# Splitting two early weight chunks in pieces and reordering the last product of a hybrid block

## The chip, the cores and the metric

The program runs on one core of a Trainium2 chip. The metric is device time in microseconds of one execution. All weights come from HBM in fp32, and the whole block is one launch.

## What is computed

One block over 256 tokens of width 2048: a SwiGLU layer of width 5632, a mixer (an S5 scan beside a gated spatial unit, with gates and an output product), and a second SwiGLU layer, each added to the residual, then a last norm:

```python
h = rms_norm(x, ffn1_norm)
x = x + 0.5 * ((silu(h @ ffn1_w_gate) * (h @ ffn1_w_up)) @ ffn1_w_down)
h = rms_norm(x, mix_norm)
...
x = x + merged @ w_out
h = rms_norm(x, ffn2_norm)
x = x + 0.5 * ((silu(h @ ffn2_w_gate) * (h @ ffn2_w_up)) @ ffn2_w_down)
return rms_norm(x, final_norm)
```

The change touches the first microseconds of the first `h @ ffn1_w_gate`, `h @ ffn1_w_up`, and the last microseconds of the last `@ ffn2_w_down` with the final norm behind it.

## The kernel before, in words

**Three products for one.** TensorE works on fp32r operands, which hold fewer bits than fp32. So each fp32 number is split into a high part (`hi`, the number rounded to fp32r) and a low part (`lo`, the rest), and a product is the sum of three matmuls: hi by hi, hi by lo, lo by hi (lines 216 to 218). The weights are split while the program runs: `split_piece` (line 147) has ScalarE (ACT) write `whi` from `raw`, and then VectorE (DVE) write `wlo` as `raw - whi`.

**Chunks.** All weights come as a list of chunks of 128 x 2048 fp32 (1 MiB) in the order in which the products use them. A chunk holds four pieces of 128 x 512. One piece with 128 rows of the input is a step of six matmuls of 512 columns: three for each half of the 256 tokens (`step`, line 212). So a chunk is 24 matmuls. There are three buffers for `raw`, three for `whi` and three for `wlo`.

**What sets the order.** Each engine works off its instructions in the order of the code. `take` (line 193) hands out one piece; ahead of each it calls `tick` (line 174), which first runs hooks set for this tick, then what is pending (`pend`, the evictions of finished products, put there by `job`, line 220), and at the first piece of a chunk calls `split_to` for the chunk two ahead, which queues that chunk's load on SP and its split on ACT and DVE.

**The start** (lines 746 to 796). The first chunk is loaded and split in four pieces, so that the first matmuls can start as soon as a quarter of it is there. The second and third chunks are split whole, between the splits of the input `xT` (`split_h1`, two of the sixteen k blocks at a time). The first eight chunks, `w1s`, hold gate and up pieces in turn, two k blocks to a chunk.

**The end** (`down_out`, line 1043). The last product has 12 k blocks (`kt`) and four column blocks of 512. Three of them run as usual, by `job`. The eviction of each (`evac`, line 1053) is on DVE an addition to `x_sb` (line 294) and two products with the last norm's gain (line 1051), and on ACT two sums of squares (line 273); the third also loads ACT's table for the square root (line 1061). The fourth column block is taken in one go, all 12 pieces first (line 1067); then for each token half `h` come its 36 matmuls (lines 1072 to 1074), the addition (line 1076), its square, gain and norm, and the stores. Both halves' sums stand in one accumulator tile `acc` of 128 x 2 x 512; the pool `ps` has three such tiles.

Of the kernel before, what the change touches and what calls it, by code (L numbers as in the profile page):

```python
# [13 lines left out]
ALU = mybir.AluOpType  # L14
# [12 lines left out]
SUB = 2048  # L27
# [18 lines left out]
def f(ap):  # L46
    return ap.bitcast(F32)
# [3 lines left out]
def kernel(  # L51
# [31 lines left out]
    act, dve, pe, pool = nc.scalar, nc.vector, nc.tensor, nc.gpsimd  # L83
# [55 lines left out]
    def load_to(i):  # L139
        while st["load"] <= min(i, NSUB - 1):  # L140
            j = st["load"]
            t = wp.tile([P, SUB], F32, tag="raw", name="raw", bufs=NRAW)
            nc.sync.dma_start(out=t, in_=chunks[j])
            raws[j] = t
            st["load"] += 1

    def split_piece(hi, lo, r, s):
        act.activation(out=hi[:, s], in_=r[:, s], func=AF.Copy)  # L148
        dve.tensor_tensor(out=lo[:, s], in0=r[:, s], in1=f(hi[:, s]), op=ALU.subtract)  # L149

    def split_to(i):
        while st["split"] <= min(i, NSUB - 1):
            j = st["split"]
            load_to(j + NRAW - 1)
            r = raws.pop(j)
            hi = wp.tile([P, SUB], F32R, tag="whi", name="whi", bufs=NSPL)
            lo = wp.tile([P, SUB], F32R, tag="wlo", name="wlo", bufs=NSPL)
            split_piece(hi, lo, r, slice(0, SUB))
            splits[j] = (hi, lo)
            st["split"] += 1  # L160

    pend = []
# [4 lines left out]
    def at(delta, fn):  # L167
        hooks.setdefault(st["tick"] + delta, []).append(fn)
# [5 lines left out]
    def tick():  # L174
        for fn in hooks.pop(st["tick"], ()):
            fn()
        while pend:
            pend.pop(0)()
        if st["off"] == 0:
            split_to(st["sub"] + LOOK)  # L180
            splits.pop(st["sub"] - 1, None)
        credit[0] += credit[1]
        while fillers and credit[0] >= 1.0:
            try:
                next(fillers[0])
                credit[0] -= 1.0
            except StopIteration:
                fillers.pop(0)
        if not fillers:
            credit[0] = 0.0  # L190
        st["tick"] += 1

    def take(n):
        if st["off"] % N == 0:
            tick()
        hi, lo = splits[st["sub"]]
        a = st["off"]
        st["off"] += n
        if st["off"] == SUB:
            st["off"] = 0  # L200
            st["sub"] += 1
        return hi[:, a:a + n], lo[:, a:a + n]
# [6 lines left out]
    def new_acc():  # L209
        return ps.tile([P, 2, N], F32, tag="acc", name="acc")  # L210
# [9 lines left out]
    def job(lhs, kt, evac):  # L220
        acc = new_acc()
        for k in range(kt):
            step(acc, lhs, k, k == 0, k == kt - 1)
        pend.append(lambda: evac(acc))
# [15 lines left out]
    def small():  # L240
        return ev.tile([P, 8], F32, tag="sm", name="sm", bufs=2)
# [5 lines left out]
    def split_gain(dst, src, g, k):  # L247
        act.activation(out=dst[:, 0, :], in_=src, func=AF.Copy, scale=g[:, k:k + 1])
        dve.scalar_tensor_tensor(out=dst[:, 1, :], in0=src, scalar=g[:, k:k + 1],
                                 in1=f(dst[:, 0, :]), op0=ALU.mult, op1=ALU.subtract)  # L250
# [20 lines left out]
    def square(m, h):  # L271
        j = ev.tile([P, N], BF16, tag="junk", name="junk", bufs=1)
        act.activation(out=j, in_=x_sb[:, h, m * N:m * N + N], func=AF.Square,  # L273
                       accum_out=ssq[:, h, m:m + 1])

    def rms(hs=slice(0, 2)):
        r = ev.tile([P, 2], F32, tag="rc", name="rc", bufs=2)[:, hs]
        s = small()
        n = hs.stop - hs.start
        dve.tensor_reduce(out=s[:, 0:n], in_=ssq[:, hs, :], axis=AX.X, op=ALU.add)  # L280
        rsqrt(r, s[:, 0:n], D, s[:, 2:2 + n])
        return r
# [9 lines left out]
    def add_residual(acc, m, scale):  # L292
        xs = x_sb[:, :, m * N:m * N + N]
        dve.scalar_tensor_tensor(out=xs, in0=acc, scalar=scale, in1=xs, op0=ALU.mult, op1=ALU.add)  # L294
# [477 lines left out]
    def split_h1(k0):  # L772
        for k in (k0, k0 + 1):
            split_gain(h1[:, k], xT[:, k, :], g1, k)
# [15 lines left out]
    splits[0] = (hi0, lo0)  # L790
    st["split"] = 1
    split_h1(2)
    split_to(1)
    split_h1(4)
    for i in range(5):
        at(2 + 3 * i, lambda i=i: split_h1(2 * i + 6))

# [246 lines left out]
    def down_out(gt, kt):  # L1044
        fin = hp.tile([P, 3, D], F32, tag="h", name="fin")
        xg, gf_sb = fin[:, 0:2, :], fin[:, 2, :]
        pool.dma_start(out=gf_sb, in_=gf.to_broadcast([P, D]))

        def gained(m, h):
            s = slice(m * N, m * N + N)  # L1050
            dve.tensor_tensor(out=xg[:, h, s], in0=x_sb[:, h, s], in1=gf_sb[:, s], op=ALU.mult)

        def evac(m):
            def go(acc):
                add_residual(acc, m, 0.5)
                for h in range(2):
                    square(m, h)
                for h in range(2):
                    gained(m, h)
                if m == 2:  # L1060
                    act.activation(out=small()[:, 0:1], in_=eps_t, func=AF.Sqrt)
            return go

        for m in range(3):
            job(gt, kt, evac(m))
        acc = new_acc()
        pieces = [take(N) for _ in range(kt)]
        c3 = slice(3 * N, 4 * N)
        for h in range(2):
            t = slice(h * P, h * P + P)  # L1070
            for k, (hi, lo) in enumerate(pieces):
                pe.matmul(acc[:, h, :], lhsT=gt[:, k, 0, t], rhs=hi, start=k == 0, stop=False)
                pe.matmul(acc[:, h, :], lhsT=gt[:, k, 0, t], rhs=lo, start=False, stop=False)
                pe.matmul(acc[:, h, :], lhsT=gt[:, k, 1, t], rhs=hi, start=False, stop=k == kt - 1)
            xs = x_sb[:, h, c3]
            dve.scalar_tensor_tensor(out=xs, in0=acc[:, h, :], scalar=0.5, in1=xs, op0=ALU.mult, op1=ALU.add)
            square(3, h)
            gained(3, h)
            r = rms(slice(h, h + 1))
            for i, eng in enumerate((dve, act, dve, act)):  # L1080
                o = xg[:, h, i * N:(i + 1) * N]
                if eng is dve:
                    dve.tensor_scalar(out=o, in0=o, scalar1=r, scalar2=None, op0=ALU.mult)
                    nc.sync.dma_start(out=out[:, h, i * N:(i + 1) * N], in_=o)
                else:
                    act.activation(out=o, in_=o, func=AF.Copy, scale=r)
                    act.dma_start(out=out[:, h, i * N:(i + 1) * N], in_=o)

    ffn(h3, gp2, down_out)
    gp2.release()  # L1090
    h3p.release()
# [88 lines left out]
```

## Time and profile before

| | |
|---|---|
| median of 3 runs | 2055.1 us (2053.28 to 2055.16) |
| profiled execution | 2053.59 us, its span 2051.8 us |
| mean granted TensorE clock | 0.995 |
| busy: PE, DVE, ACT, POOL | 2027.8, 1127.6, 865.0, 72.8 us |
| read from HBM | 398.21 MB, 200 GB/s over the span |

The profile is one execution. PE is TensorE's matmuls, PEld its weight loads, SP the engine whose queue issues the weights' DMAs. The granted clock is 1.00 at 2.4 GHz and 0.50 at 1.2 GHz. A row of the timeline gives the start in us from the beginning of the span, the duration, the engine and line, what is written and read, the shape, and in brackets the idle time of the engine before it with what ended it. Matmuls overlap: one lasts some 0.39 us, while the next starts some 0.23 us after it.

### The profile page before, as it was taken

The numbers are of one execution on the slowest core, as the hardware profiler recorded it, in microseconds if no ns is written. First come the engines' busy times: TensorE is split into PE (matmuls) and PEld (weight loads), VectorE is DVE, ScalarE is ACT, GpSimd is POOL, SyncE is SP. The second block draws the span as 40 slices with busy tenths as digits, with TensorE's granted clock in tenths as the row PEclk, the third lists the DMA queues.
The fourth block names the chain that finished last, engine by engine and source line by source line (L and its number), as shares of the span: only waits on it lengthen the run. The fifth ranks groups of instructions, "written<-read, shape, count | busy, mean of one in ns | idle before, by whom it ended". The sixth has DMA issues, their size and how long they took to land.

```text
span 2051.8 us, 23150 instructions
## 1 busy us (share of the span) xinstructions
PE 2027.8 (99%) x9764; PEld 1676.7 (82%) x9764; DVE 1127.6 (55%) x1102; ACT 865.0 (42%) x705; POOL 72.8 (4%) x134
## 2 busy tenths in 40 slices
PE   9999999999999999989999999999999999999997
PEld 7888888888888888878888888888888888888886
DVE  5765565555664555546765665544444444444454
ACT  6543334444334454434435444533433443333343
POOL 0000000111000000011100000000000000000000
PEclk9999999999999999999999999999999999999999
DMA  7557665565665455557765455555555555555552
GB/s 310 198 195 226 231 240 209 196 216 204 209 208 192 174 195 198 213 178 247 236 227 210 175 185 188 210 187 186 193 196 185 190 188 197 186 200 188 185 190 98
DMA packets 66489, 412.20 MB, mean 201 GB/s; under 512 B 10272, under 2 KB 10928, under 8 KB 20560
## 3 DMA queue, kind: packets, MB, share of 16 engines
q1 hardware_dynamic: 53280, 378.56, 52.0%
q0 software_dynamic: 10656, 27.93, 4.3%
q10 hardware_dynamic: 2448, 4.22, 0.6%
q8 instruction: 76, 1.25, 0.2%
q14 instruction: 29, 0.24, 0.0%
HBM read 398.21 MB, written 12.45 MB: 200 GB/s over the span
## 4 chain that ended last, share of the span: by engine, by line
PE 97%; DVE 1%; ACT 1%; issue 1%; DMA 0%; SPq 0%; ACTq 0%
PE acc L216 31%; PE acc L218 30%; PE acc L217 30%; PE q L258 2%; ACT whi L148 1%; PE q L588 0%; PE q L724 0%; PE acc L234 0%; PE acc L233 0%; PE acc L232 0%; DMA raw<-in_w1s_dram 0%; DVE wlo L149 0%; PE q L681 0%; PE q L885 0%; PE q L721 0%
## 5 line engine op out<-in xcount | busy, mean ns | idle before, releaser
L149 DVE TENSOR_TENSOR wlo<-raw,whi 128x2048 fp32r<-128x2048 f32 (+1 forms) x359 | 815.7, 2274 | 810.2 <-ACT whi L148 810.0
L148 ACT ACTIVATE whi<-raw 128x2048 fp32r<-128x2048 f32 (+1 forms) x359 | 682.2, 1901 | 913.2 <-PE acc L218 835.0
L216 PE MATMUL acc<-whi,h 128*128 128x512 f32 x1856 | 728.0, 392 | 1.2 <-ACT whi L148 1.2
L217 PE MATMUL acc<-wlo,h 128*128 128x512 f32 x1856 | 723.8, 390 | 2.2 <-DVE wlo L149 2.0
L218 PE MATMUL acc<-whi,h 128*128 128x512 f32 x1856 | 723.4, 390 | 0.0
L217 PEld LDWEIGHTS acc<-wlo,h 128*128 128x128 f32 x1856 | 349.2, 188 | 74.3 <-DVE wlo L149 3.2
L216 PEld LDWEIGHTS acc<-whi,h 128*128 128x128 f32 x1856 | 349.1, 188 | 74.2 <-ACT whi L148 1.6
L218 PEld LDWEIGHTS acc<-whi,h 128*128 128x128 f32 x1856 | 349.1, 188 | 73.0
L216 PE MATMUL acc<-whi,gt 128*128 128x512 f32 x680 | 266.1, 391 | 0.0
L218 PE MATMUL acc<-whi,gt 128*128 128x512 f32 x680 | 266.1, 391 | 0.0
L217 PE MATMUL acc<-wlo,gt 128*128 128x512 f32 x680 | 265.1, 390 | 0.0
L217 PEld LDWEIGHTS acc<-wlo,gt 128*128 128x128 f32 x680 | 127.7, 188 | 27.6
L218 PEld LDWEIGHTS acc<-whi,gt 128*128 128x128 f32 x680 | 127.7, 188 | 27.1
L216 PEld LDWEIGHTS acc<-whi,gt 128*128 128x128 f32 x680 | 127.7, 188 | 26.6
L319 ACT ACTIVATE t<-acc,rc 128x512 f32<-128x512 f32 x44 | 27.9, 686 | 63.4 <-PE acc L218 63.4
L216 PE MATMUL acc<-whi,mT 128*128 128x512 f32 x128 | 50.2, 392 | 0.0
L294 DVE SCALAR_TENSOR_TENSOR x_sb<-acc,x_sb 128x1024 f32<-128x1024 f32 x27 | 33.1, 1225 | 30.9 <-PE acc L218 30.9
L218 PE MATMUL acc<-whi,mT 128*128 128x512 f32 x128 | 49.9, 389 | 0.0
L217 PE MATMUL acc<-wlo,mT 128*128 128x512 f32 x128 | 49.8, 389 | 0.0
L273 ACT ACTIVATE junk<-x_sb 128x512 bf16<-128x512 f32 x32 | 20.2, 631 | 66.2 <-DVE x_sb L294 53.0
L329 DVE SCALAR_TENSOR_TENSOR t<-acc,rc,t 128x512 f32<-128x512 f32 x44 | 31.0, 745 | 16.8 <-PE acc L218 16.8
L244 ACT ACTIVATE gt<-q 128x512 fp32r<-128x512 f32 x44 | 23.9, 596 | 29.1 <-PE q L258 29.1
(200 smaller groups left out, 1067.3 us busy)
## 6 DMA issues: line engine op xcount, KB each, us to landing
raw<-in_w1d_dram SPq DMA_DIRECT2D x44, 1024.0 KB, 4.9
raw<-in_w2g_dram SPq DMA_DIRECT2D x44, 1024.0 KB, 4.8
raw<-in_w2u_dram SPq DMA_DIRECT2D x44, 1024.0 KB, 4.8
raw<-in_w2d_dram SPq DMA_DIRECT2D x44, 1024.0 KB, 4.8
raw<-in_w1g_dram SPq DMA_DIRECT2D x40, 1024.0 KB, 4.8
raw<-in_w1u_dram SPq DMA_DIRECT2D x40, 1024.0 KB, 4.9
raw<-in_w_in_dram SPq DMA_DIRECT2D x24, 1024.0 KB, 4.8
raw<-in_w_gb_dram SPq DMA_DIRECT2D x16, 1024.0 KB, 5.3
```

The source lines that it names most:

```text
L148: act.activation(out=hi[:, s], in_=r[:, s], func=AF.Copy)
L149: dve.tensor_tensor(out=lo[:, s], in0=r[:, s], in1=f(hi[:, s]), op=ALU.subtract)
L216: pe.matmul(acc[:, h, :], lhsT=lhs[:, k, 0, t], rhs=hi, start=first, stop=False)
L217: pe.matmul(acc[:, h, :], lhsT=lhs[:, k, 0, t], rhs=lo, start=False, stop=False)
L218: pe.matmul(acc[:, h, :], lhsT=lhs[:, k, 1, t], rhs=hi, start=False, stop=last)
L244: act.activation(out=dst[:, :, 0, :], in_=src, func=AF.Copy)
L258: pe.transpose(q[:, i, h * P:h * P + P], src[:, h, c:c + P], ident)
L273: act.activation(out=j, in_=x_sb[:, h, m * N:m * N + N], func=AF.Square, accum_out=ssq[:, h, m:m + 1])
L294: dve.scalar_tensor_tensor(out=xs, in0=acc, scalar=scale, in1=xs, op0=ALU.mult, op1=ALU.add)
L319: act.activation(out=s[:, h, :], in_=acc[:, h, :], func=AF.Silu, scale=rc(h))
L329: dve.scalar_tensor_tensor(out=s[:, h, :], in0=acc[:, h, :], scalar=rc(h), in1=s[:, h, :], op0=ALU.mult, op1=ALU.mult)
```

## The change

`split_to` gets a number of parts. The second chunk is split in four parts of 512 columns, the third in two of 1024 (its call now stands ahead of the first product; before, the first tick made it, at the same place of the order). In the last product, the eviction of the third column block is taken out of `pend` while the twelve pieces are taken, and run behind them. Each token half gets an accumulator tile of its own.

```diff
--- before.py
+++ after.py
@@ -148,14 +148,16 @@
         act.activation(out=hi[:, s], in_=r[:, s], func=AF.Copy)
         dve.tensor_tensor(out=lo[:, s], in0=r[:, s], in1=f(hi[:, s]), op=ALU.subtract)
 
-    def split_to(i):
+    def split_to(i, parts=1):
         while st["split"] <= min(i, NSUB - 1):
             j = st["split"]
             load_to(j + NRAW - 1)
             r = raws.pop(j)
             hi = wp.tile([P, SUB], F32R, tag="whi", name="whi", bufs=NSPL)
             lo = wp.tile([P, SUB], F32R, tag="wlo", name="wlo", bufs=NSPL)
-            split_piece(hi, lo, r, slice(0, SUB))
+            w = SUB // parts
+            for p in range(parts):
+                split_piece(hi, lo, r, slice(p * w, p * w + w))
             splits[j] = (hi, lo)
             st["split"] += 1
 
@@ -790,8 +792,9 @@
     splits[0] = (hi0, lo0)
     st["split"] = 1
     split_h1(2)
-    split_to(1)
+    split_to(1, 4)
     split_h1(4)
+    split_to(2, 2)
     for i in range(5):
         at(2 + 3 * i, lambda i=i: split_h1(2 * i + 6))
 
@@ -1063,17 +1066,21 @@
 
         for m in range(3):
             job(gt, kt, evac(m))
-        acc = new_acc()
+        late = list(pend)
+        pend.clear()
         pieces = [take(N) for _ in range(kt)]
+        for fn in late:
+            fn()
         c3 = slice(3 * N, 4 * N)
         for h in range(2):
             t = slice(h * P, h * P + P)
+            acc = new_acc()[:, 0, :]
             for k, (hi, lo) in enumerate(pieces):
-                pe.matmul(acc[:, h, :], lhsT=gt[:, k, 0, t], rhs=hi, start=k == 0, stop=False)
-                pe.matmul(acc[:, h, :], lhsT=gt[:, k, 0, t], rhs=lo, start=False, stop=False)
-                pe.matmul(acc[:, h, :], lhsT=gt[:, k, 1, t], rhs=hi, start=False, stop=k == kt - 1)
+                pe.matmul(acc, lhsT=gt[:, k, 0, t], rhs=hi, start=k == 0, stop=False)
+                pe.matmul(acc, lhsT=gt[:, k, 0, t], rhs=lo, start=False, stop=False)
+                pe.matmul(acc, lhsT=gt[:, k, 1, t], rhs=hi, start=False, stop=k == kt - 1)
             xs = x_sb[:, h, c3]
-            dve.scalar_tensor_tensor(out=xs, in0=acc[:, h, :], scalar=0.5, in1=xs, op0=ALU.mult, op1=ALU.add)
+            dve.scalar_tensor_tensor(out=xs, in0=acc, scalar=0.5, in1=xs, op0=ALU.mult, op1=ALU.add)
             square(3, h)
             gained(3, h)
             r = rms(slice(h, h + 1))
```

Line numbers of the changed kernel are higher by 2 or 3, near the end by 7.

ACT at the start. `whi` are the high parts; `h_130` is the split input.

```order
L248 ACTIVATE h_130<-xT,vec_sb 128x256 x2
L148 ACTIVATE whi<-raw 128x2048
L248 ACTIVATE h_130<-xT,vec_sb 128x256 x2
L148 ACTIVATE whi<-raw 128x2048
L248 ACTIVATE h_130<-xT,vec_sb 128x256 x2
L148 ACTIVATE whi<-raw 128x2048
```

The same place of ACT's order in the changed kernel:

```order
L250 ACTIVATE h_130<-xT,vec_sb 128x256 x2
L148 ACTIVATE whi<-raw 128x512 x4
L250 ACTIVATE h_130<-xT,vec_sb 128x256 x2
L148 ACTIVATE whi<-raw 128x1024 x2
L250 ACTIVATE h_130<-xT,vec_sb 128x256 x2
L148 ACTIVATE whi<-raw 128x2048
```

The places are the same, and the same pieces stand on DVE for `wlo`. The fourth chunk is still split whole.

ACT at the end of the program: `junk,ssq` are the squares, `sm` is the one-element square root that goes with the table.

```order
L148 ACTIVATE whi<-raw 128x2048 x3
L273 ACTIVATE junk,ssq<-x_sb 128x512 x2
L1061 ACT_TABLE_LOAD
L1061 ACTIVATE sm<-eps_t 128x1
L148 ACTIVATE whi<-raw 128x2048
L273 ACTIVATE junk,ssq<-x_sb 128x512
L262 ACTIVATE rc<-sm,eps_t 128x1
```

The same place of ACT's order in the changed kernel:

```order
L148 ACTIVATE whi<-raw 128x2048 x4
L275 ACTIVATE junk,ssq<-x_sb 128x512 x2
L1064 ACT_TABLE_LOAD
L1064 ACTIVATE sm<-eps_t 128x1
L275 ACTIVATE junk,ssq<-x_sb 128x512
L264 ACTIVATE rc<-sm,eps_t 128x1
```

The last chunk's split moved ahead of the squares and the table load. On DVE it likewise moved ahead of the third block's addition and its two gain products.

PE where the second token half of the fourth column block begins, with the semaphores waited for. Before:

```order
L1072 MATMUL acc<-whi,gt 128x512
L1073 MATMUL acc<-wlo,gt 128x512
L1074 MATMUL acc<-whi,gt 128x512
L1072 MATMUL acc<-whi,gt 128x512 [waits DVE_49]
L1073 MATMUL acc<-wlo,gt 128x512
L1074 MATMUL acc<-whi,gt 128x512
```

The same six matmuls on PE in the changed kernel:

```order
L1079 MATMUL acc<-whi,gt 128x512
L1080 MATMUL acc<-wlo,gt 128x512
L1081 MATMUL acc<-whi,gt 128x512
L1079 MATMUL acc<-whi,gt 128x512 [waits PE_49]
L1080 MATMUL acc<-wlo,gt 128x512
L1081 MATMUL acc<-whi,gt 128x512
```

The second half's first matmul waited for DVE; it now waits for a count of PE's own.

## Rows read from the trace of the kernel before

**Rows 1.** page, part 1 (busy us, share of the span, instructions)

```profile
PE 2027.8 (99%) x9764; PEld 1676.7 (82%) x9764; DVE 1127.6 (55%) x1102; ACT 865.0 (42%) x705; POOL 72.8 (4%) x134
```

**Rows 2.** waits of PE (us in total, times, longest us)

```profile
PE acc L217 <- DVE wlo L149: 2.0, 2, 1.8
PE acc L216 <- ACT whi L148: 1.2, 1, 1.2
PE acc L1073 <- DVE wlo L149: 1.8, 1, 1.8
PE acc L1072 <- ACT whi L148: 0.8, 1, 0.8
PE acc L1072 <- DVE x_sb L1076: 0.8, 1, 0.8
```

**Rows 3.** timeline of ACT and DVE, first 28 us (start us, us, engine, line, operation)

```profile
4.79 0.63 ACT L148 ACTIVATE whi<-raw 128x512 fp32r<-128x512 f32 x1 [1.06 <-DMA raw<-in_w1s_dram]
6.60 1.97 ACT L148 ACTIVATE whi<-raw 128x512 fp32r<-128x512 f32 x3
11.35 1.91 ACT L148 ACTIVATE whi<-raw 128x2048 fp32r<-128x2048 f32 x1 [1.60 <-DMA raw<-in_w1s_dram]
14.52 1.91 ACT L148 ACTIVATE whi<-raw 128x2048 fp32r<-128x2048 f32 x1 [0.45 <-DMA raw<-in_w1s_dram]
20.25 1.92 ACT L148 ACTIVATE whi<-raw 128x2048 fp32r<-128x2048 f32 x1 [3.03 <-DMA raw<-in_w1s_dram]
...
5.46 0.69 DVE L149 TENSOR_TENSOR wlo<-raw,whi 128x512 fp32r<-128x512 f32 x1 [1.21 <-ACT whi L148]
7.27 2.03 DVE L149 TENSOR_TENSOR wlo<-raw,whi 128x512 fp32r<-128x512 f32 x3 [0.29 <-ACT whi L148]
13.29 2.29 DVE L149 TENSOR_TENSOR wlo<-raw,whi 128x2048 fp32r<-128x2048 f32 x1 [3.02 <-ACT whi L148]
22.20 2.29 DVE L149 TENSOR_TENSOR wlo<-raw,whi 128x2048 fp32r<-128x2048 f32 x1 [2.66 <-ACT whi L148]
26.00 2.28 DVE L149 TENSOR_TENSOR wlo<-raw,whi 128x2048 fp32r<-128x2048 f32 x1
```

**Rows 4.** timeline of PE, first 30 us

```profile
11.78 0.39 PE L218 MATMUL acc<-whi,h 128*128 128x512 f32 x1
15.64 0.80 PE L217 MATMUL acc<-wlo,h 128*128 128x512 f32 x1 [1.82 <-DVE wlo L149]
28.20 0.39 PE L217 MATMUL acc<-wlo,h 128*128 128x512 f32 x1
```

**Rows 5.** busy time by stretch (PE, PEld, DVE, ACT, POOL, PEclk, DMA share, GB/s)

```profile
16.00:17.00 1.00, 1.00 (x3) 0.81 (x3) 0.92 (x2) 1.00 (x3) 0.00 (x0) 0.50 1.03 430
2030.00:2031.00 1.00, 1.00 (x3) 0.81 (x3) 0.00 (x0) 0.00 (x0) 0.00 (x0) 0.50 0.00 0
2034.00:2035.00 1.00, 0.28 (x1) 0.28 (x2) 0.97 (x2) 0.24 (x1) 0.00 (x0) 1.00 0.00 0
```

**Rows 6.** timeline of ACT, DVE and PE at the end of the program

```profile
2025.41 1.90 ACT L148 ACTIVATE whi<-raw 128x2048 fp32r<-128x2048 f32 x1
...
2021.19 1.23 DVE L294 SCALAR_TENSOR_TENSOR x_sb<-acc,x_sb 128x1024 f32<-128x1024 f32 x1 [1.20 <-PE acc L218]
2027.34 2.29 DVE L149 TENSOR_TENSOR wlo<-raw,whi 128x2048 fp32r<-128x2048 f32 x1 [3.60 <-ACT whi L148]
...
2026.21 0.39 PE L1074 MATMUL acc<-whi,gt 128*128 128x512 f32 x1
2033.55 0.39 PE L1074 MATMUL acc<-whi,gt 128*128 128x512 f32 x1
2034.72 0.50 PE L1072 MATMUL acc<-whi,gt 128*128 128x512 f32 x1 [0.78 <-DVE x_sb L1076]
2037.14 0.39 PE L1073 MATMUL acc<-wlo,gt 128*128 128x512 f32 x1
2042.81 0.39 PE L1074 MATMUL acc<-whi,gt 128*128 128x512 f32 x1
```

## The prediction

> **What bounds the kernel now.** I read the page first. PE is busy 99% of the span [rows 1]. The matmuls are the same in number and size in both kernels, so a change of order can only win back time in which PE stands still or is slow. The list of PE's waits shows where it stands still [rows 2]: beside the mixer, which the change doesn't touch, two places, and both are edited. At the start PE waited 1.2 us for `whi` and up to 1.8 us at once for `wlo` (lines 216, 217). At the end it waited 0.8 us for `whi`, 1.8 us for `wlo` and 0.8 us for DVE's addition to `x_sb` (lines 1072, 1073). That is 6.4 us. The stretches of busy time then show what follows such a wait [rows 5]: at 16 us and at 2030 us the granted clock is 0.50, the lower level (1.2 GHz), after PE had done almost nothing for some 3.5 us (11.78 to 15.64, 2026.21 to 2029.69, the second one from the end of DVE's split below). At 2034 us, behind the wait of 0.8 us, it is 1.00. The rest is read from the timelines [rows 3, 4, 6].
>
> The pace of matmuls at the full clock: from 2037.14 to 2042.81 there are 25 starts [rows 6], so 5.67 / 25 = 0.227 us each; a chunk of 24 takes 5.44 us.
>
> **Start, second chunk in four parts.** Its load lands at 11.35, which ends ACT's wait [rows 3]. Whole, `whi` takes 1.91 us and `wlo` ends at 13.29 + 2.29 = 15.58; PE goes on at 15.64. In parts, the first chunk gives the prices: a 512-wide part is 0.63 us on ACT and 0.69 us on DVE, and in a row three cost 1.97 and 2.03 us, 0.66 and 0.68 each [rows 3]. So the first `whi` part is there at 11.98, its `wlo` at 12.02 + 0.69 = 12.71, and PE's second matmul of the chunk starts at 12.76 in place of 15.64. The parts follow every 0.68 us while PE needs six matmuls (1.36 us) for each, so it waits for none of the others. The four together cost DVE some 0.43 us more than the whole (2.72 against 2.29), but `wlo` ends at 14.75 and not at 15.58, as DVE starts earlier.
>
> PE stands idle only between about 12.3 and 12.76, and the slow stretch behind it should go.
>
> **Third chunk in two parts.** The trace has no 1024-wide part. The bounds are the 512-wide and the 2048-wide one, 0.63 and 1.91 us on ACT, 0.69 and 2.29 on DVE; on the line between them it is 1.06 and 1.22 us. ACT is through with the second chunk at 13.95 and with two 256-wide input blocks (at most two 512-wide parts, 1.26 us; I take 0.9, an estimate) at 14.85; the third chunk is there at 14.52 [rows 3]. So `whi` of its first part is ready by 15.95 and `wlo` by 17.2. PE comes there at 12.76 + 23 x 0.23 = 18.1. With the upper bounds of both engines `wlo` would be there at 14.85 + 1.91 + 2.29 = 19.1, a wait of 0.8 us, which the next step would take in whole.
>
> **What is late next: the fourth chunk.** It is still split whole, and its load lands at 20.25, which ended ACT's wait there too [rows 3]. In rows 5 the DMA share is 1.03 at 430 GB/s around 16 us: the queues are full at the start, and the issue of this load hangs on the first chunk only, which the change leaves alone. So `wlo` is ready at 22.20 + 2.29 = 24.49 as before. PE would be there at 18.1 + 24 x 0.227 = 23.55 for the first and 23.78 for the second matmul; the second can't start before 24.55. That is a new wait of 0.8 us where there was none. Before, this second matmul started at 28.20 [rows 4]. Gain: 28.20 - 24.55 = 3.65 us, less 0.15 for the slower pace of the first matmuls after a wait (2034.72 to 2037.14 is 10 starts, 2.42 us against 2.27), so **3.5 us**. If the load came a little earlier, up to 4.4 us (27.98 by the same count, less 23.55). Of the 3.5 us, the slow stretch is 28.20 - 15.64 - 48 x 0.227 = 1.7 us. The fifth chunk's `wlo` starts at 26.00 and ends at 28.28 [rows 3]; PE now needs it at 29.6: no wait. Behind that the splits wait for PE, not PE for them.
>
> **End, the last split ahead of the third eviction.** Before, the addition to `x_sb` starts at 2021.19 [rows 6], when PE has finished the third column block. The same event frees the buffers for the last chunk, but its split stands behind the addition, the squares and the table load, and starts at 2025.41 on ACT and at 2027.34 on DVE. Put first, it starts at 2021.19 and is through at 2023.1 on ACT and, 2.29 us later, at 2025.45 on DVE. PE needs `whi` one start after 2026.21, at 2026.44, and `wlo` at 2026.66, so 1.2 us are to spare. From 2026.21 to 2033.55 there are 12 starts, 2.72 us at full pace; they took 7.34. Gain **4.6 us**: 2.6 of waits, 2.0 of the slow clock and restart.
>
> What waits for the moved eviction: DVE adds from 2025.45 in place of 2021.19, 4.26 us later, so ACT's squares, table load and root end at some 2025.41 + 4.26 = 2029.7. The first half's addition comes at about 2029.4 and its square at 2030.1. It just fits; if not, the first half's norm is late, and that has the second half's 8.2 us of matmuls to hide in.
>
> **One accumulator per half.** The second half's first matmul starts 1.17 us after the last one of the first half [rows 6], 0.94 us more than the pace, and 0.15 us go in the restart. The new tile is that of the second column block, evicted long ago, so the wait goes: **1.1 us**. The wait for PE's own count could cost from nothing to one matmul's overlap, 0.39 - 0.23 = 0.16 us; I take nothing, as it counts matmuls of that earlier block. From the last matmul (2042.81) to the end nothing changes.
>
> **Sum.** 3.5 + 4.6 + 1.1 = 9.2 us. The profiled execution took 2053.59 us, its span 2051.8: 2044.4. It lies 1.5 us under the median shown. The four executions known average 2054.3, so I say **2045.1 us**.
>
> The slow clock's price, 1.7 and 2.0 us, is from one execution. The Trainium skill (TensorE: Matmul & The Clock Gate, "What's actually happening") says that the number of slow matmuls varies from run to run, 6, 11 or 14 for one kernel. By that, with 11 as the middle, the two prices together would be 2.0 to 4.7 us in place of 3.7 (an estimate), and the sum 7.5 to 10.2. The trace shows two such stretches with nearly one price, so I stay with it.
>
> **Rivals.**
> - *The clock falls all the same* (10%). Both short waits at the start, 0.5 and 0.8 us, are still there. If one puts PE at the lower level, one slow stretch of 1.7 to 2.0 us stays: 2047.0. Against it: the wait of 0.8 us at 2034 us left the clock at 1.00 [rows 5]. The same page (section "A second HAM failure mode: psum-queue depth-cycling") has short idles between groups of matmuls bring it down again and again.
> - *The start's gain is swallowed* (10%). Later loads, or work in the mixer that waits for transfers, don't come earlier, and PE waits 3.5 us more there: 2045.1 + 3.5 = 2048.6. For it: the DMA queues are full at the start. Against it: PE uses 1 MiB in 5.44 us, 193 GB/s, under half of the 430 in rows 5, so loads catch up.
> - *The end doesn't do what it says* (4%). The first half would get the tile of the third block, and would wait for its late addition until 2026.7, 5.7 us from 2021.0; that eats the whole 5.7 us of the end: 2054.3 - 3.5 = 2050.8. Against it: three tiles in turn give it that of the first block.
> - *Slower* (3%). The clock stays low behind the new wait at 23.8 us. Each matmul then costs 0.2 us more (512 columns at 1.2 GHz are 0.427 us, against 0.227), so the gain is gone after 46 matmuls and the time is over 2058 after 67. At 100 of them: 2065. Against it: both slow stretches were over after 1.7 to 2.0 us of loss, some 8 to 10 matmuls.
>
> **How the numbers follow.** The forecast as worked out has 73%. The range takes in the first two rivals and the bounds: low is the lowest execution less the full 4.4 + 5.7 us, 2053.28 - 10.1 = 2043.2, high the highest less the end's 5.7 alone, 2055.16 - 5.7 = 2049.5. A measurement here can tell about 0.2%, 4.1 us, from no change. Forecast and the first two rivals are faster by more: 93% with it, less 1 for unlucky runs; the third rival and those runs are the same, 5%; slower 3%.
>
> **What would show it.** Right: the wait for `wlo` on line 1073's successor and for `x_sb` gone; the stretches at 16 us and 2030 us at clock 1.00; one wait of some 0.8 us at the fourth chunk's `wlo`, near 24 us; last matmul some 9 us earlier. Wrong: a stretch at 0.50 behind 24 us, a first matmul of the fourth column block that waits for DVE, or mixer waits longer than before.

## The result and the profile after

The changed kernel takes **2044.86 us** (median of 6 runs, 2044.27 to 2045.82) beside 2054.54 us (median of 6) before: a ratio of 0.995 with an interval of 0.9937 to 0.9963, so 0.4 to 0.6% faster. The profiled execution took 2044.42 us, its span 2042.6 us, 9.2 less than before. Work is the same, 9764 matmuls in both; PE has lost waits and slow stretches. First the page's part 1, to be read beside [rows 1]:

```profile
PE 2024.2 (99%) x9764; PEld 1675.0 (82%) x9764; DVE 1127.6 (55%) x1106; ACT 865.1 (42%) x709; POOL 72.5 (4%) x134
```

Then the list of PE's waits (us in total, times, longest us). Of the five waits in [rows 2], the three at the end are gone. At the start the wait for `whi` is down to 0.3 us. The line for `wlo` holds two waits: the old one at the second chunk, down from 1.8 to 0.2 us, and a new one of 0.6 us at the fourth chunk, both seen in the timeline below:

```profile
PE acc L219 <- DVE wlo L149: 0.8, 2, 0.6
PE acc L218 <- ACT whi L148: 0.3, 1, 0.3
```

The timeline of ACT, DVE and PE at the start, which answers to [rows 3, 4]:

```profile
11.27 2.19 ACT L148 ACTIVATE whi<-raw 128x512 fp32r<-128x512 f32 x4 [1.75 <-DMA raw<-in_w1s_dram]
14.42 2.01 ACT L148 ACTIVATE whi<-raw 128x1024 fp32r<-128x1024 f32 x2 [0.15 <-DMA raw<-in_w1s_dram]
20.17 1.92 ACT L148 ACTIVATE whi<-raw 128x2048 fp32r<-128x2048 f32 x1 [2.94 <-DMA raw<-in_w1s_dram]
...
11.94 2.50 DVE L149 TENSOR_TENSOR wlo<-raw,whi 128x512 fp32r<-128x512 f32 x4 [1.90 <-ACT whi L148]
15.51 2.36 DVE L149 TENSOR_TENSOR wlo<-raw,whi 128x1024 fp32r<-128x1024 f32 x2 [0.29 <-ACT whi L148]
22.12 2.29 DVE L149 TENSOR_TENSOR wlo<-raw,whi 128x2048 fp32r<-128x2048 f32 x1 [3.45 <-ACT whi L148]
...
12.68 0.50 PE L219 MATMUL acc<-wlo,h 128*128 128x512 f32 x1 [0.23 <-DVE wlo L149]
23.47 0.39 PE L218 MATMUL acc<-whi,h 128*128 128x512 f32 x1
24.46 0.50 PE L219 MATMUL acc<-wlo,h 128*128 128x512 f32 x1 [0.60 <-DVE wlo L149]
```

The second chunk's first low half is there at 12.6, and PE's second matmul of that chunk starts at 12.68 (15.64 before). It comes to the fourth chunk at 23.47, but starts its second matmul there at 24.46: the low half is written from 22.12 on, in one piece. That is the one wait that is new.

The stretches of busy time, after [rows 5] (last columns PEclk, DMA share, GB/s). The clock is 1.00 where it was 0.50, and stays so over the new wait; at 2024 us PE is busy without a break:

```profile
16.00:17.00 1.00, 1.00 (x6) 0.84 (x5) 1.00 (x2) 1.00 (x3) 0.00 (x0) 1.00 1.03 430
24.00:25.00 1.00, 0.54 (x2) 0.49 (x3) 1.00 (x3) 1.00 (x1) 0.00 (x0) 1.00 1.03 434
2024.00:2026.00 2.00, 2.00 (x11) 1.65 (x10) 0.54 (x2) 1.97 (x4) 0.00 (x0) 1.00 0.00 0
```

The end, after [rows 6]:

```profile
2017.75 1.92 ACT L148 ACTIVATE whi<-raw 128x2048 fp32r<-128x2048 f32 x1 [3.52 <-PE acc L220]
2024.66 1.28 ACT L1064 ACT_TABLE_LOAD   x1
2026.70 0.63 ACT L275 ACTIVATE junk<-x_sb 128x512 bf16<-128x512 f32 x1 [0.54 <-DVE x_sb L1083]
...
2019.70 2.29 DVE L149 TENSOR_TENSOR wlo<-raw,whi 128x2048 fp32r<-128x2048 f32 x1 [3.15 <-ACT whi L148]
2021.91 1.22 DVE L296 SCALAR_TENSOR_TENSOR x_sb<-acc,x_sb 128x1024 f32<-128x1024 f32 x1
2025.91 0.69 DVE L1083 SCALAR_TENSOR_TENSOR x_sb<-acc,x_sb 128x512 f32<-128x512 f32 x1 [1.46 <-PE acc L1081]
...
2022.99 0.39 PE L1079 MATMUL acc<-whi,gt 128*128 128x512 f32 x1
2025.48 0.39 PE L1081 MATMUL acc<-whi,gt 128*128 128x512 f32 x1
2025.71 0.39 PE L1079 MATMUL acc<-whi,gt 128*128 128x512 f32 x1
2033.64 0.39 PE L1081 MATMUL acc<-whi,gt 128*128 128x512 f32 x1
```

The last split starts on ACT at 2017.75, when the third column block is done, and its low half ends at 2021.99. PE reaches it at 2022.99, one start later for `wlo`, and doesn't wait. The second half's first matmul (2025.71) starts 0.23 us after the last one of the first half (2025.48).

How much each place gave is read from marks that both traces have. Two rows of the chain that ended last, before:

```profile
369.84 1.41 DVE t L329 x2
...
1002.10 0.70 DVE y L650
```

and after:

```profile
366.23 1.41 DVE t L331 x2
...
998.80 0.69 DVE y L652
```

The first mark lies behind the start, ahead of the mixer: 369.84 - 366.23 = 3.6 us earlier. At the second, in the mixer, it is 1002.10 - 998.80 = 3.3. The event that frees the last split came at 2021.19 and comes at 2017.75, 3.4 us earlier; the last matmul came at 2042.81 and comes at 2033.64, 9.2 earlier. So the start gave 3.6 us, the stretch between took 0.2 back, and the end gave 5.7.

### The profile page after: what moved, and what is told of

Read it like the earlier page. It is cut to its first block, busy times and chain, and to the rows that moved or that the text cites. A ratio compares the mean times of both kernels' runs of the same rounds, so it can differ in the third digit from the quotient of the medians.

```text
span 2042.6 us, 23157 instructions
## 1 busy us (share of the span) xinstructions
PE 2024.2 (99%) x9764; PEld 1675.0 (82%) x9764; DVE 1127.6 (55%) x1106; ACT 865.1 (42%) x709; POOL 72.5 (4%) x134
## 4 chain that ended last, share of the span: by engine, by line
PE 97%; DVE 1%; DMA 1%; ACT 1%; issue 1%; SPq 0%; ACTq 0%
PE acc L218 31%; PE acc L220 30%; PE acc L219 30%; PE q L260 2%; DMA raw<-in_w1s_dram 1%; ACT whi L148 1%; PE q L590 0%; PE q L726 0%; PE acc L236 0%; PE acc L235 0%; PE acc L234 0%; PE q L683 0%; PE acc L1081 0%; PE acc L1079 0%; DVE wlo L149 0%
```

## The experiments

All medians in us; "before" was run beside each.

| run | edit | median (range) | before beside it | ratio, interval |
|---|---|---|---|---|
| e1 | start alone | 2050.72 (2049.87 to 2052.13) | 2054.02 | 0.9984, 0.9975 to 0.9994 |
| e2 | end alone | 2048.72 (2046.75 to 2050.38) | 2054.02 | 0.9971, 0.9960 to 0.9982 |
| e3 | one accumulator again | 2046.06 (2044.79 to 2047.03) | 2054.02 | 0.9959, 0.9944 to 0.9974 |
| e4 | fourth chunk in two, too | 2044.57 (2043.20 to 2044.72) | 2054.02 | 0.9951, 0.9936 to 0.9965 |
| e5 | third chunk whole | 2045.15 (2044.75 to 2045.74) | 2054.78 | 0.9955, 0.9940 to 0.9970 |
| e6 | second chunk in two | 2045.17 (2044.69 to 2045.65) | 2054.78 | 0.9955, 0.9940 to 0.9970 |
| e7 | old order, last chunk in four | 2045.19 (2044.64 to 2045.65) | 2054.78 | 0.9955, 0.9939 to 0.9972 |
| e8 | before, waits filled | 2052.61 (2051.93 to 2056.25) | 2054.78 | 0.9993, 0.9984 to 1.0002 |
| e9 | the change again | 2044.39 (2044.13 to 2045.31) | 2054.83 | 0.9953, 0.9940 to 0.9965 |
| e10 | e4 again | 2044.07 (2043.12 to 2044.89) | 2054.83 | 0.9950, 0.9936 to 0.9964 |

**e1, the start alone.** The changed kernel with the old end:

```diff
-        late = list(pend)
-        pend.clear()
+        acc = new_acc()
         pieces = [take(N) for _ in range(kt)]
-        for fn in late:
-            fn()
```

and `acc[:, h, :]` for the halves.

> The changed kernel with the end of before: only the second and third chunk in parts. Theory: the start's gain stands alone, some 3.5 us, so before less 3.5 (2050.5 to 2051.0 beside 2054.3); the end shows its three waits (0.8, 1.8, 0.8 us) and the slow stretch unchanged. Rival 1, the start's gain is swallowed later and the 9.2 us come from the end: as before, 2054. Rival 2, start and end are tied through the clock: anything clearly below 2050.

Measured: 2050.72, 3.3 us under before in the same job. PE's waits in this run:

```profile
PE acc L1076 <- DVE wlo L149: 1.8, 1, 1.8
PE acc L219 <- DVE wlo L149: 1.1, 1, 1.1
PE acc L1075 <- DVE x_sb L1079: 0.8, 1, 0.8
PE acc L1075 <- ACT whi L148: 0.8, 1, 0.8
```

The three at the end (lines 1075, 1076) are those of before; the 1.1 us on line 219 are the new wait at the fourth chunk, whose split started at 20.48 here. The gain at the start is not swallowed later: rival 1 is out. Nothing points to rival 2 either, as the median is not below 2050.

**e2, the end alone.** Before, with the change's last block in `down_out`.

> Before with the end of the change: the last split ahead of the third eviction and one accumulator per half; the start whole. Theory: before less 5.7 us, 2048.4 to 2048.8; the start shows its waits of 1.2 and 1.8 us and the granted clock of 0.50 behind 15.6 us. Rival (all gain at the end): 2045.

Measured: 2048.72, 5.3 us under before and not at the rival's 2045. PE's waits at the start:

```profile
PE acc L216 <- ACT whi L148: 2.6, 1, 2.6
PE acc L217 <- DVE wlo L149: 1.8, 1, 1.8
```

The wait for `whi` is 2.6 us here, 1.2 in [rows 2], as the second chunk's load landed 0.8 us later in this execution (12.16 against 11.35) and PE was through with the first chunk 0.6 us sooner (its last matmul started at 11.16, against 11.78 in [rows 4]):

```profile
11.16 0.39 PE L218 MATMUL acc<-whi,h 128*128 128x512 f32 x1
...
16.44 0.79 PE L217 MATMUL acc<-wlo,h 128*128 128x512 f32 x1 [1.82 <-DVE wlo L149]
```

And the slow stretch behind it is longer; three stretches of busy time, PEclk third from the end:

```profile
18.00:19.00 1.00, 1.00 (x4) 0.81 (x3) 1.00 (x1) 0.23 (x1) 0.00 (x0) 0.50 1.00 418
20.00:21.00 1.00, 1.00 (x4) 0.78 (x3) 0.55 (x2) 0.00 (x0) 0.00 (x0) 0.50 0.96 401
21.00:22.00 1.00, 1.00 (x4) 0.81 (x3) 0.00 (x0) 0.74 (x1) 0.00 (x0) 0.50 0.87 336
```

In the profile of before the stretch at 19 us was already at 1.00. Between the second chunk's second matmul, 16.44, and the mark ahead of the mixer, 371.84, this run took 355.40 us; before took 369.84 - 15.64 = 354.20. So the slow stretch cost 1.2 us more here. The stall ahead of it was also 1.4 us longer, and no run shows how much of the 1.2 us comes from that and how much is chance. e1 and e2 together give 3.3 + 5.3 = 8.6 us, against 9.2 between the spans and 9.7 between the medians of the first comparison: they add up, within what their ranges leave open.

**e3, one accumulator for both halves again.**

```diff
+        both = new_acc()
         for h in range(2):
             t = slice(h * P, h * P + P)
-            acc = new_acc()[:, 0, :]
+            acc = both[:, h, :]
```

> The changed kernel with both token halves in one accumulator tile again. Theory: the second half waits 0.8 us for the first half's addition to x_sb, as before, so 1.1 us slower than the change, about 2046.0, and the wait is the only difference. Rival: the wait was the late DVE queue's doing (DVE had been behind with the last split), so with the split moved it is gone anyway: no difference, 2044.9.

Measured: 2046.06, 1.2 us over the first median of the change, 1.7 over its second (e9), with ranges that overlap. The trace is sharper. The wait is back, at its old size:

```profile
PE acc L1080 <- DVE x_sb L1084: 0.8, 1, 0.8
```

From the last matmul of the first half to the last of the second it is 2036.22 - 2026.96 = 9.26 us here, and 2033.64 - 2025.48 = 8.16 in the change: 1.1 us, as expected. So the wait came from the shared tile and not from a late DVE, and the separate tiles are needed beside the new order.

**e4 and e10, the fourth chunk in two parts; e9, the change once more.** In `tick`:

```diff
-            split_to(st["sub"] + LOOK)
+            split_to(st["sub"] + LOOK, 2 if st["sub"] == 1 else 1)
```

> The changed kernel with the fourth chunk split in two parts as well. Theory: what bounds the start now is the fourth chunk's split in one piece, 1.92 + 2.29 us behind its landing at 20.2. In two parts the first low half is there at 20.2 + 1.0 + 1.2 = 22.4, ahead of PE (23.7): the wait of 0.6 us goes, with its slow first matmuls 0.7 to 0.9 us faster than the change, about 2044.1. Rival: the load itself bounds the start (DMA share 1.0 up to 36 us), so the wait only moves to the fifth or sixth chunk: no difference, 2044.9.

> The changed kernel once more, as the other side of the next run on the same chip. Theory: 2044.9, its wait for the fourth chunk's low half 0.4 to 0.8 us, depending on when that chunk's load lands (20.2 to 20.9 in the profiles so far).

> The fourth chunk in two parts once more, beside the changed kernel on the same chip. Theory: 0.7 to 0.9 us faster than the change in the median of five rounds, with no wait at the fourth chunk. Rival: the wait's place is taken by later loads or by the mixer, whose long wait for the gated unit doesn't move in step: within 0.3 us of the change.

In e9 the wait at the fourth chunk is 0.6 us, as in the first profile of the change. In e4 and e10 it is gone; what is left is at the second one:

```profile
PE acc L219 <- DVE wlo L149: 0.2, 1, 0.2
```

To compare starts across executions, whose loads land at different times, take the first mark less the start of the fourth chunk's `whi` on ACT, which its load releases:

| run | fourth chunk's split starts | first mark | between |
|---|---|---|---|
| before | 20.25 | 369.84 | 349.59 |
| e2, end alone | 21.26 | 371.84 | 350.58 |
| e8, waits filled | 20.93 | 368.99 | 348.06 |
| the change | 20.17 | 366.23 | 346.06 |
| e9, the change again | 20.49 | 366.55 | 346.06 |
| e1, start alone | 20.48 | 366.57 | 346.09 |
| e3, one accumulator | 20.70 | 366.77 | 346.07 |
| e7, old order, four parts | 20.25 | 366.32 | 346.07 |
| e5, third chunk whole | 20.92 | 367.03 | 346.11 |
| e6, second chunk in two | 20.36 | 366.52 | 346.16 |
| e4, fourth chunk in two | 20.28 | 365.46 | 345.18 |
| e10, the same again | 20.60 | 365.82 | 345.22 |

Seven executions with parts at the start and a whole fourth chunk have the same 346.1 us to within 0.1, whenever the load lands: the start hangs on that chunk. In two parts it is 0.9 us shorter, twice, as expected. There PE no longer waits for the fourth chunk, only for the second; counted from the start of the second chunk's split (11.41 and 11.72) it is 354.05 and 354.10 us to the mark, against 354.96 and 354.94 in the change and e9 (11.27 and 11.61), so the 0.9 us are the same by either load. But the medians show only 0.3 us (2044.57 against 2044.86, 2044.07 against 2044.39), with ranges that overlap, where 0.7 to 0.9 was expected. What can take such a gain away again is seen in the mixer. PE stands still there for 4.6 us in every kernel, and the slow stretch behind that varies. In e9 PE goes on at 873.11, in e10 at 872.39. Two stretches of e9:

```profile
878.00:879.00 1.00, 1.00 (x5) 0.76 (x5) 0.61 (x3) 0.00 (x0) 0.00 (x0) 0.79 0.05 16
879.00:880.00 1.00, 1.00 (x6) 0.82 (x5) 0.00 (x0) 0.00 (x0) 0.00 (x0) 1.00 0.00 0
```

and of e10, whose start was 0.7 us ahead at the first mark and whose span is 0.5 us longer:

```profile
878.00:879.00 1.00, 1.00 (x4) 0.80 (x3) 0.00 (x0) 0.00 (x0) 0.00 (x0) 0.50 0.00 0
879.00:880.00 1.00, 1.00 (x4) 0.71 (x3) 0.00 (x0) 0.00 (x0) 0.00 (x0) 0.50 0.00 0
```

Behind the same wait, three of the 512-column matmuls start some 0.4 us or more apart in e9, and nine in e10, where 0.23 is the usual pace. At the second mark e10 (998.90) is 0.5 us behind e9 (998.43): it has lost 1.2 us in between. Whether the mixer is also what holds the medians together is not shown, as each run has a trace of one execution only. So that this version beats the change is shown at the start, by 0.9 us, and not by the whole time.

**e5, the third chunk whole.** `split_to(2)` in place of `split_to(2, 2)`.

> The changed kernel with the third chunk split whole, the second still in four parts. Theory: its low half comes at some 18.7 in place of 16.7, PE waits about 0.4 us for it at the third chunk, and the wait at the fourth chunk takes that in, as the fourth chunk's split ends at 24.4 either way: no difference, 2044.9. Rival: each edit counts for itself, 0.4 to 0.7 us slower, 2045.5.

Measured: 2045.15, and 346.11 in the table above. PE waits at the third chunk (19.48; 0.7 us, where about 0.4 was expected), and so has next to no wait left at the fourth (25.22, behind 24.87):

```profile
19.48 0.50 PE L219 MATMUL acc<-wlo,h 128*128 128x512 f32 x1 [0.69 <-DVE wlo L149]
...
24.87 0.39 PE L218 MATMUL acc<-whi,h 128*128 128x512 f32 x1
25.22 0.50 PE L219 MATMUL acc<-wlo,h 128*128 128x512 f32 x1
```

The one wait took in the other. The third chunk's two parts brought nothing here.

**e6, the second chunk in two parts.** `split_to(1, 2)` in place of `split_to(1, 4)`.

> The changed kernel with the second chunk in two parts in place of four. Theory: its first low half comes 0.9 us later (13.55), PE waits that much more there and no more at the fourth chunk; the clock stays at 1.00 over the longer wait: 0 to 0.2 us slower, 2044.9 to 2045.1. Rival: PE then stands still for longer, the clock falls to the lower level there, 1.5 us slower or more: 2046.5.

Measured: 2045.17, and 346.16. PE's two waits at the second chunk are longer, 0.38 and 0.77 us:

```profile
12.60 0.49 PE L218 MATMUL acc<-whi,h 128*128 128x512 f32 x1 [0.38 <-ACT whi L148]
13.86 0.50 PE L219 MATMUL acc<-wlo,h 128*128 128x512 f32 x1 [0.77 <-DVE wlo L149]
```

and the clock behind them is still 1.00 (the column before the DMA share):

```profile
14.00:15.00 1.00, 1.00 (x5) 0.82 (x6) 1.00 (x2) 0.65 (x2) 0.00 (x0) 1.00 1.05 426
```

So two parts do nearly what four do; the fourth chunk sets the time in both.

**e7, the end in its old order, with the last chunk in four parts.** No `late`; in `tick`, `split_to(st["sub"] + LOOK, 4 if st["sub"] + LOOK == NSUB - 1 else 1)`.

> The changed kernel with the end's old order (third eviction, squares and table load first), but the last chunk split in four parts behind them. Theory: only the lateness of the last low half counts, not the order: ACT starts at 4.2 us behind the eviction's release, the first parts are there after 1.4 us more, when PE needs them; a wait of 0.1 to 0.3 us is left, 2045.1. Rival: the order itself matters (ACT or DVE is delayed by the eviction for longer, or PE waits for each part): 1 us or more slower, 2046 or above.

Measured: 2045.19. ACT starts the split where the table load ends, 4.2 us behind the release, and PE loses 0.38 - 0.23 = 0.15 us between its first and second matmul of the chunk, and 0.1 more in the restart:

```profile
2022.13 2.18 ACT L148 ACTIVATE whi<-raw 128x512 fp32r<-128x512 f32 x4
...
2023.15 0.39 PE L1075 MATMUL acc<-whi,gt 128*128 128x512 f32 x1
2023.53 0.50 PE L1076 MATMUL acc<-wlo,gt 128*128 128x512 f32 x1
```

So it is the lateness of the last low half that cost 4.6 us, and either edit removes it, all but some 0.25 us here: the split first, or its first quarter soon.

**e8, before with the waits filled.** Before, and in the first step of the second chunk:

```diff
+        for _ in range(fill[0] if fill else 0):
+            pe.matmul(idle[:, :P], lhsT=ident, rhs=ident, start=True, stop=True)
...
+            for _ in range(fill[1] if fill and h == 0 else 0):
+                pe.matmul(idle[:, :P], lhsT=ident, rhs=ident, start=True, stop=True)
```

with three and four.

> Before, with seven 128x128 fp32 matmuls on the identity put into PE's two waits at the second chunk (three ahead of its first matmul, four behind it; their result is not used). The waits stay, PE is busy in them. Theory: the slow stretch behind 15.6 us comes from PE's standing still; with PE busy the granted clock there is 1.00, and the time is 1.7 us less than before, 2052.4 beside 2054.0. Rival: the slow pace there has another cause (the waits themselves, the full DMA queues): clock 0.50 again, no gain, 2054.0 or more.

Measured: 2052.61 beside 2054.78, with a ratio whose interval (0.9984 to 1.0002) doesn't exclude no change. The trace is clearer. The fillers (each of the seven shows as two records) cover part of the waits, which stay (PE goes on at 16.34, as late as the load makes it):

```profile
12.03 0.83 PE L215 MATMUL idle<-ident 128*128 128x128 f32 x6
14.35 1.05 PE L220 MATMUL idle<-ident 128*128 128x128 f32 x8
16.34 0.50 PE L221 MATMUL acc<-wlo,h 128*128 128x512 f32 x1 [0.94 <-DVE wlo L149]
```

and the granted clock behind is 1.00, where it was 0.50 in [rows 5]:

```profile
17.00:18.00 1.00, 1.00 (x6) 0.82 (x5) 0.91 (x2) 0.94 (x3) 0.00 (x0) 1.00 0.97 401
```

From that second matmul to the first mark it is 368.99 - 16.34 = 352.65 us, against 354.20 before: 1.55 us, of the 1.7 expected. The slow stretch comes from PE's standing still and not from the full DMA queues, whose share in the row is 0.97. The other slow stretch, at 2030 us in [rows 5], had no DMA at all.

## Why the prediction was right

**The start, second and third chunk.** The first low half was forecast for 12.71 and PE's second matmul for 12.76; it started at 12.68, with the load 0.08 us earlier and the first part at the prices read from the first chunk. All four parts took 2.19 us on ACT and 2.50 on DVE, less than the 2.61 and 2.72 of the forecast; PE waited only for the first, so that changed nothing. The two 1024-wide parts, between 0.63 and 1.91 us on ACT and 0.69 and 2.29 on DVE, took 2.01 and 2.36 us for both, beside 2.12 and 2.44 on the line between the ends.

**The fourth chunk.** The new wait of 0.8 us was forecast for a second matmul at 24.55; it started at 24.46, since the load landed 0.08 us earlier. Gain 3.6 us at the first mark, forecast 3.5. That this chunk alone sets the start is shown by the table of e5, e6, e4. The third chunk's parts weren't needed for the sum. The upper bounds of the forecast are the price of the whole split, and what the text said of them, that the next wait would take such a loss in, is what e5 shows.

**The end.** Forecast 4.6 + 1.1 = 5.7 us, measured 5.7. ACT was through with the moved eviction at 2026.2 and stood idle for 0.54 us before the first half's square: it fits, with as little to spare as forecast. The wait for PE's own count cost nothing (0.23 us from start to start). e7 adds that the order is one of two ways.

**The clock.** Forecast to stay up over waits of 0.5 and 0.8 us: it did, and in e6 over 0.4 and 0.8 close together. The rival of a falling clock is out for this kernel. The price of the slow stretch at the start, 1.7 us in the profile of before, was 1.55 by e8; that of the stretch at the end, 2.0 us, has no run of its own and is part of the 4.6 that went there. A slow stretch can cost more: e2's is 1.2 us dearer behind a longer stall, and the mixer's differ by 1.2 us between e9 and e10 behind the same wait. The Trainium skill (TensorE: Matmul & The Clock Gate, "What's actually happening") says that the number of slow matmuls at the start of one kernel varies from run to run; the traces of the mixer agree, with three in e9 and nine in e10. With the stall at the start gone the spread is smaller too: sixteen runs of before in the job of e1 lie over 4.1 us (2051.98 to 2056.07), eleven of the change over 1.7 (2044.13 to 2045.82). But the ten of e8, which keeps the waits, lie over 4.3 us, so how much of the spread is the clock's is not shown.

**The sum.** 9.2 us forecast, 9.2 between the spans; 2045.1 against 2044.86. That it fits to a tenth is luck: the medians give 9.7 us here and 10.4 in the job of e9 (2054.83 against 2044.39). What the sum left out is the mixer: from the first mark to the second it took 632.26 us in before and 632.57 in the change, with no edit to it, and 1.2 us more in e10 than in e9. The prediction's "two places" also passed over two waits of PE in the list of before: 1.4 us of the warm-up matmuls (line 750) and 0.7 us for `t` (line 329). The change has both at the same size, so no term is missing. The mixer's few tenths were small beside 9.2. Beside e4's 0.9 us its 1.2 us is not, and there my expectation of the median failed.

## What to carry to other kernels

Where the busiest engine stands still at the ends of a program, follow each wait to the one piece of work that comes late and ask what is late behind it: here the third chunk's two parts (e5) and the second chunk's four parts in place of two (e6) gave next to nothing of their own, since the fourth chunk's load and whole split set the time. A late operand can be cured by moving its work ahead in the queue or by cutting it so that its first part comes soon; both were worth nearly the same here (4.6 us, and 0.25 less). A stall on TensorE costs its length and can cost a slow stretch behind it: here 1.7 and 2.0 us behind two stalls of some 3.5 us in which PE did almost nothing, and none behind the new wait at the fourth chunk, even where it was 1.1 us (e1, clock 1.00 at 24 us and after). So removing most of 6.4 us of waits gave 9.2.

## What the runs showed of the hardware

- **Loads land at different times.** In the twelve profiles the fourth chunk's split, released by its load, starts between 20.17 and 21.26 us; from 11 to 21 us the DMA share is 1.01 to 1.03 in each. Where the start hangs on that load, its whole time moves with it, so marks less the landing compare better (within 0.1 us) than runs (1 to 2 us from the lowest to the highest).
- **The slow stretch has no fixed length.** In the mixer, behind the same wait of 4.6 us, the clock was back at 1.00 by 879 us in e9 (PE went on at 873.11) and still at 0.50 from 879 to 880 us in e10 (872.39), which made 1.2 us. At the second chunk it was back by 19 us in before and not by 22 us in e2, behind a longer stall. So an edit worth about 1 us can't be told from the medians of a few runs.
